# Sums for the second feed-forward products formed during the first ones, stored and loaded into place

## The chip, the cores and the metric

The kernel runs on one core of a Trainium2 chip. The metric is the device time of one execution in microseconds (us). Engines are named as in the profile: PE (TensorE matmul), PEld (its weight load), DVE (VectorE), ACT (ScalarE), POOL (GpSimd), SP (SyncE, which here only issues transfers). A name ending in q (SPq, DVEq) is an engine's queue of instructions.

## The reference, cut to what matters

Two transformer blocks follow each other on 1024 tokens of width 1024, in fp32. Each ends in a gated feed-forward network, and only these two networks are touched here. `D_FF` is 2816.

```python
def _swiglu(h, w_ffn_in, w_ffn_out):
    a, g = jnp.split(h @ w_ffn_in, 2, axis=-1)
    return (jax.nn.silu(g) * a) @ w_ffn_out
...
        x = x + g2 * _swiglu(_modulate(_rmsnorm(x, norm2_g[l]), sh2, sc2), w_ffn_in[l], w_ffn_out[l])
```

## The kernel before

**Products.** Every fp32 product is made of three fp32r matmuls: an operand x is split into a high part (a cast, made by ACT at L192) and a low part (x minus the high part, made by DVE or POOL at L193), and high by high, high by low and low by high are added in PSUM. PSUM has eight banks, used in turn, four named `mm` and four named `ax`. A 512-token product of one 128-row column is 128x512 in size; q is 0 or 1 for the two halves of the tokens.

**First products** (`ffn_in`, L1021). The hidden width is 22 columns f of 128 rows. A column and its gate form a 2x2 block product by Strassen's scheme in Winograd's form: seven products of 12 matmuls, in the order B11, T2, T1, T3, T4, B21, B22, with sums of weights on DVE (`total`, L1036) and sums of results on DVE (L1123 to L1129). `hidden` (L1072) multiplies the two factors into one 128x512 tile for each f and q, and `store` and `flush` (L220, L225) put it out to the DRAM tensor `hid` on SP's queue, 44 stores in each feed-forward.

**Second products** (`ffn_out`, L1132). The 22 columns are taken in five blocks, `FF_BLOCKS = (("P", 3), ("W", 6), ("P", 3), ("W", 6), ("P", 4))`. A P block is plain: 16 products of 3 (or 4) columns, 9 matmuls each for three columns. A W block is again Strassen-Winograd over six columns, in three pairs (k, k+3): 28 products of 9 matmuls (L1270 to L1272), seven for each pair of output rows m. P blocks evacuate PSUM with ACT (the first block, L1316) or with a DVE addition into x (L1281, in the second feed-forward L1279); W blocks with DVE (L1325 to L1333, L1281) and some with POOL.

**Operands of the second products.** A generator prepares each block's operands during the block before; `tick` runs it one step per product. For a P block it is `plain` (L1143): load a tile of `hid` (L1149), split it. For a W block it is `forms` (L1155). It loads the pair's four tiles b11, b12, b21, b22 into temporaries (L1169) and forms, on DVE except for T3 on POOL,

```python
T1 = b12 - b11    # L1179      T3 = b22 - b12   # L1180, POOL
T2 = b22 - T1     # L1182      T4 = T2 - b21    # L1187
```

and splits B11, B21, B22 and T1 to T4 into the parts that the matmuls read: `half` tiles for B11 and most of B21, the pool `hl` of 32 buffers for the rest. So W block 1 is prepared in P block 0, and W block 3 in P block 2. The weights of the second products are loaded by `unit` (L148, split at L150 and L151) or, for W blocks, by `supply` (loads L1233, DVE sums L1243 to L1246, splits L192 and L193). During W block 3, `residue` adds the residual from DRAM on DVE (L1288); during W block 1 of the first feed-forward some constants of the attention are made (`extra`, L1531 to L1541).

**Order.** Each engine runs its instructions in order. A list scheduler decides that order when the kernel is built, so a queue's order can differ from the order of the code.

## Time and profile before

| | us |
|---|---|
| median of 3 runs | 3383.36 (3383.23 to 3383.85) |
| the profiled execution | 3384.4 |
| its span | 3382.5 |
| PE busy in it | 3238.6 (96%) |
| DVE, POOL, ACT busy | 2135.1, 1533.4, 1357.7 |
| first feed-forward: first products, then the five blocks | from about 1191, 1622 to 1867 |
| second feed-forward: first products, then the five blocks | from about 2684, 3115 to the end |

PE is busy nearly always, so what can be won without taking away matmuls is the time in which it waits or runs at less than its usual pace. "Busy" counts instructions from start to end, and matmuls overlap; how many matmuls ran in a stretch, beside how long it is, shows more than the busy share. All times below count from the start of the span.

### The profile page before, as it was taken

What the parts mean: (1) busy time and instruction counts of PE and PEld (TensorE: products, weight loads), DVE (VectorE), ACT (ScalarE), POOL (GpSimd) and SP (SyncE); (2) the same over time, 40 slices, a digit from 0 to 9 for tenths busy, and PEclk for the clock granted to TensorE, in tenths of its full rate; (3) what the DMA queues carried; (4) which work ended last, traced back from release to release, by engine and by line L of the source; (5) the groups of instructions that cost most, each with busy time, mean ns of one, the idle gap of its engine ahead of it and who ended that gap; (6) DMA issues with size and microseconds to landing.
All of it is one profiled execution on the core that took longest, in us unless ns stands there. A gap on an engine that the chain in (4) does not pass through costs nothing. (4 is left out here: it accounts for less than half of the span.)

```text
span 3382.5 us, 43295 instructions
## 1 busy us (share of the span) xinstructions
PE 3238.6 (96%) x15868; PEld 2690.6 (80%) x15868; DVE 2135.1 (63%) x3438; ACT 1357.7 (40%) x2394; POOL 1533.4 (45%) x991
## 2 busy tenths in 40 slices
PE   7989999999999999999999999999999999999988
PEld 4779888888988878888777878787877878888767
DVE  7563234234577386555698578778776586564786
ACT  4552122221122342323433377767675332232433
POOL 3213233231322685454565534444445675544865
PEclk8989999999999999999999999999999999999999
DMA  7121111244237422221443411112114422222342
GB/s 272 60 103 54 63 57 60 75 163 152 79 100 234 154 84 99 78 78 68 129 138 118 133 33 52 55 47 63 58 50 147 143 100 94 87 78 94 101 139 72
DMA packets 153012, 335.11 MB, mean 99 GB/s; under 512 B 20864, under 2 KB 29184, under 8 KB 152800
## 3 DMA queue, kind: packets, MB, share of 16 engines
q1 hardware_dynamic: 140640, 311.36, 27.8%
q10 hardware_dynamic: 12160, 20.98, 1.7%
q8 instruction: 126, 2.06, 0.3%
q14 instruction: 86, 0.70, 0.1%
HBM read 263.07 MB, written 69.21 MB: 98 GB/s over the span
## 5 line engine op out<-in xcount | busy, mean ns | idle before, releaser
L151 POOL TENSOR_TENSOR wl<-raw,wh 128x1024 fp32r<-128x1024 f32 (+1 forms) x188 | 421.9, 2247 | 707.9 <-ACT wh L150 645.9
L163 PE MATMUL mm<-hl,wh 128*128 128x512 f32 (+1 forms) x1584 | 629.8, 398 | 1.4 <-ACT t L1567 1.4
L164 PE MATMUL mm<-hl,wh 128*128 128x512 f32 (+1 forms) x1584 | 618.9, 391 | 0.0
L165 PE MATMUL mm<-hl,wl 128*128 128x512 f32 (+1 forms) x1584 | 618.5, 390 | 0.0
L193 POOL TENSOR_TENSOR wl<-half,wh 128x512 fp32r<-128x512 f32 x308 | 431.7, 1424 | 346.8 <-ACT wh L192 341.5
L150 ACT CAST wh<-raw 128x1024 fp32r<-128x1024 f32 (+3 forms) x189 | 177.1, 939 | 453.4 <-PE mm L164 340.8
L165 PEld LDWEIGHTS mm<-hl,wl 128*128 128x128 f32 (+1 forms) x1584 | 297.2, 188 | 64.3
L163 PEld LDWEIGHTS mm<-hl,wh 128*128 128x128 f32 (+1 forms) x1584 | 297.7, 188 | 59.3 <-ACT t L1567 1.8
L164 PEld LDWEIGHTS mm<-hl,wh 128*128 128x128 f32 (+1 forms) x1584 | 298.0, 188 | 56.7 <-issue 0.5
L192 ACT CAST wh<-half 128x512 fp32r<-128x512 f32 x308 | 178.5, 618 | 392.0 <-PE ax L1058 197.1
L1036 DVE TENSOR_TENSOR half<-half 128x512 f32<-128x512 f32 x176 | 204.4, 1201 | 3.0
L1626 POOL TENSOR_SCALAR p<-p,ast 128x384 f32<-128x384 f32 (+1 forms) x64 | 82.5, 1289 | 240.4 <-DVE ast L1624 160.9
L175 PE MATMUL mm<-wh,hl 128*128 128x256 f32 x576 | 165.2, 287 | 0.0
L176 PE MATMUL mm<-wh,hl 128*128 128x256 f32 x576 | 163.7, 285 | 0.8 <-DVE hl L193 0.6
L177 PE MATMUL mm<-wl,hl 128*128 128x256 f32 x576 | 163.5, 284 | 0.0
L1058 PE MATMUL mm<-hl,wh 128*128 128x512 f32 x360 | 140.5, 390 | 3.3 <-POOL hl L193 3.3
L1057 PE MATMUL mm<-hl,wh 128*128 128x512 f32 x360 | 140.3, 390 | 0.7 <-ACT hl L192 0.7
L1059 PE MATMUL mm<-hl,wl 128*128 128x512 f32 x360 | 140.1, 389 | 0.0
L1057 PE MATMUL ax<-hl,wh 128*128 128x512 f32 x344 | 134.2, 390 | 2.1 <-ACT hl L192 1.3
L1059 PE MATMUL ax<-hl,wl 128*128 128x512 f32 x344 | 134.1, 390 | 0.1
L1058 PE MATMUL ax<-hl,wh 128*128 128x512 f32 x344 | 133.9, 389 | 0.0
L193 POOL TENSOR_TENSOR wl<-raw,wh 128x384 fp32r<-128x384 f32 x96 | 120.1, 1273 | 17.9 <-ACT wh L192 17.9
(412 smaller groups left out, 7992.4 us busy)
## 6 DMA issues: line engine op xcount, KB each, us to landing
half<-in_w_fi SPq DMA_DIRECT2D x196, 256.0 KB, 4.8
hid<-t SPq DMA_DIRECT2D x78, 256.0 KB, 2.0
half<-hid SPq DMA_DIRECT2D x72, 256.0 KB, 4.9
raw<-in_w_ada SPq DMA_DIRECT2D x32, 512.0 KB, 3.8
raw<-in_w_o SPq DMA_DIRECT2D x32, 512.0 KB, 3.7
raw<-in_w_fo SPq DMA_DIRECT2D x32, 384.0 KB, 3.8
slot<-in_w_ada SPq DMA_DIRECT2D x16, 512.0 KB, 10.2
raw<-in_w_u SPq DMA_DIRECT2D x16, 512.0 KB, 3.9
```

Source lines behind the costliest of these rows:

```text
L150: nc.scalar.copy(hi, r)
L151: self.last_split = (eng or nc.gpsimd).tensor_tensor(lo, r, hi.bitcast(F32), op=ALU.subtract).ins
L163: mm(o, wh[:, k], h[k][q][:, s], start=k == 0, stop=False)
L164: mm(o, wh[:, k], l[k][q][:, s], start=False, stop=False)
L165: mm(o, wl[:, k], h[k][q][:, s], start=False, stop=k == kt - 1)
L175: mm(o, h[k][q][:, s], wh[:, k % 4], start=k == 0, stop=False)
L192: self.nc.scalar.copy(hi, x)
L193: (eng or self.nc.vector).tensor_tensor(lo, x, hi.bitcast(F32), op=ALU.subtract)
L1036: V.tensor_tensor(s, a, b, op=op)
L1057: mm(o, wh[:, k], h, start=k == 0, stop=False)
L1058: mm(o, wh[:, k], l, start=False, stop=False)
L1059: mm(o, wl[:, k], h, start=False, stop=k == 3)
```

## The change

`ffn_in` now takes the columns of a W block pair by pair (3 and 6, 4 and 7, 5 and 8, then 12 and 15 and so on: `order`), keeps the four tiles of a pair, and as soon as the second column is done forms T1, T2 and T4 on DVE and T3 on POOL. These sums go to a new DRAM tensor `sums`. All stores of hidden tiles and sums are issued by ACT, one per product, at least one entry behind (`due`); b12 of a pair isn't stored, since only the sums use it. `forms` no longer adds anything: it loads B11, B21, B22 and T1 to T4 straight into the buffers of their low parts, and `split` takes the high part from there and then the low part in place. The pool of `half` tiles grows from 44 to 47 buffers. The products, their operands and their number stay the same (15273 PE instructions in both programs), as do the counts of DVE and POOL instructions (3440 and 996). DMAs issued by ACT rise by 124, those of SP fall from 954 to 902.

```diff
--- before.py
+++ after.py
@@ -1018,7 +1018,7 @@
                 nc.scalar.dma_start(self.xs[m][:, hs(q)], x[m][q])
             self.bg.append(norm(q, acc))
 
-    def ffn_in(self, wi, hid):
+    def ffn_in(self, wi, hid, sums):
 
 
         nc = self.nc
@@ -1026,9 +1026,20 @@
         add, sub = ALU.add, ALU.subtract
         nf = FT
 
+        order, pair, f0 = [], {}, 0
+        for kind, n in FF_BLOCKS:
+            if kind == "W":
+                for k in range(n // 2):
+                    order += [f0 + k, f0 + n // 2 + k]
+                    pair[f0 + n // 2 + k] = f0 + k
+            else:
+                order += range(f0, f0 + n)
+            f0 += n
+        held, due = {}, deque()
+
         def load(f, i, j):
             r = self.half()
-            nc.sync.dma_start(r, wi[2 * f + i][:, hs(j)])
+            nc.sync.dma_start(r, wi[2 * order[f] + i][:, hs(j)])
             return r
 
         def total(a, b, op):
@@ -1050,6 +1061,8 @@
         def product(w, n):
             mm = nc.tensor.matmul
             self.tick()
+            if len(due) > 1:
+                nc.scalar.dma_start(*due.popleft())
             banks[0] += 1
             o = self.mm_bank() if banks[0] % 2 else self.ax_bank()
             wh, wl = w
@@ -1070,8 +1083,21 @@
             return s
 
         def hidden(f, q, s, c):
+
             V.tensor_tensor(s, s, c, op=ALU.mult)
-            self.store(hid[f][:, hs(q)], s)
+            f = order[f]
+            held[f, q] = s
+            if not (f in pair.values() and q):
+                due.append((hid[f][:, hs(q)], s))
+            if f in pair and q:
+                g = pair[f]
+                b11, b12, b21, b22 = (held.pop(k) for k in ((g, 0), (g, 1), (f, 0), (f, 1)))
+                t1, t2, t4 = (self.half() for _ in range(3))
+                V.tensor_tensor(t1, b12, b11, op=sub)
+                nc.gpsimd.tensor_tensor(b12, b22, b12, op=sub)
+                V.tensor_tensor(t2, b22, t1, op=sub)
+                V.tensor_tensor(t4, t2, b21, op=sub)
+                due.extend((sums[g][i], t) for i, t in enumerate((t1, t2, b12, t4)))
 
         raws, todo, ready = {}, [], deque()
         seen = [0]
@@ -1128,8 +1154,10 @@
             hidden(f, 0, s0, u3)
             V.tensor_tensor(u2, u2, product(weights(), "B22"), op=add)
             hidden(f, 1, gate(u2), c22)
-
-    def ffn_out(self, wo, hid, xs, scale, pieces, squares, norm, extra=lambda: iter(())):
+        while due:
+            nc.scalar.dma_start(*due.popleft())
+
+    def ffn_out(self, wo, hid, sums, xs, scale, pieces, squares, norm, extra=lambda: iter(())):
 
 
 
@@ -1162,33 +1190,33 @@
                     X[nm].append((new(F32R), new(F32R)))
 
             def load(k):
-                B = []
-                for f in (k, n + k):
-                    for q in QS:
-                        B.append(self.t512() if k % 2 else self.half())
-                        nc.sync.dma_start(B[-1], hid[f0 + f][:, hs(q)])
-                return B
-            B = [load(k) for k in range(min(n, 2))]
+
+                for nm, f, q in (("B11", k, 0), ("B22", n + k, 1), ("B21", n + k, 0)):
+                    nc.sync.dma_start(X[nm][k][1].bitcast(F32), hid[f0 + f][:, hs(q)])
+                    if nm == "B22":
+                        nc.sync.dma_start(X["T1"][k][1].bitcast(F32), sums[f0 + k][0])
+                for i, nm in ((1, "T2"), (2, "T3"), (3, "T4")):
+                    nc.sync.dma_start(X[nm][k][1].bitcast(F32), sums[f0 + k][i])
+
+            def parts(k, nm, eng=None):
+                hi, lo = X[nm][k]
+                self.split(hi, lo, lo.bitcast(F32), eng=eng)
+            for k in range(min(n, 2)):
+                load(k)
             yield
             for k in range(n):
-                b11, b12, b21, b22 = B.pop(0)
-                parts = lambda nm, t, eng=None: self.split(*X[nm][k], t, eng=eng)
-                parts("B11", b11)
-                parts("B22", b22, nc.gpsimd)
+                parts(k, "B11")
+                parts(k, "B22", nc.gpsimd)
                 yield
-                V.tensor_tensor(b11, b12, b11, op=sub)
-                nc.gpsimd.tensor_tensor(b12, b22, b12, op=sub)
-                parts("T1", b11)
-                V.tensor_tensor(b22, b22, b11, op=sub)
+                parts(k, "T1")
                 yield
-                parts("B21", b21)
-                parts("T2", b22)
+                parts(k, "B21")
+                parts(k, "T2")
                 yield
-                V.tensor_tensor(b21, b22, b21, op=sub)
-                parts("T3", b12, nc.gpsimd)
-                parts("T4", b21)
+                parts(k, "T3", nc.gpsimd)
+                parts(k, "T4")
                 if k + 2 < n:
-                    B.append(load(k + 2))
+                    load(k + 2)
                 yield
 
         def block(bi):
@@ -1351,15 +1379,16 @@
 
     def ffn(self, wi, wo, *a):
         hid = self.dram(f"hid{self.loads}", [FT, P, T])
-        self.ffn_in(wi, hid)
-        self.ffn_out(wo, hid, self.xs, *a)
+        sums = self.dram(f"sums{self.loads}", [FT, 4, P, HQ])
+        self.ffn_in(wi, hid, sums)
+        self.ffn_out(wo, hid, sums, self.xs, *a)
 
     def block1(self):
         with ExitStack() as ctx:
             self.banks(ctx, 4, 4, "1")
             self.ap = self.pool(ctx, "ada", 2)
             self.phase_a()
-            self.gp = self.pool(ctx, "halves1", 44)
+            self.gp = self.pool(ctx, "halves1", 47)
             a = self.spatial()
             self.merge1(*a)
             self.lru_consts()
@@ -1792,7 +1821,7 @@
         self.mixers()
         with ExitStack() as ctx:
             self.banks(ctx, 4, 4, "3")
-            self.gp = self.pool(ctx, "halves2", 44)
+            self.gp = self.pool(ctx, "halves2", 47)
             self.merge2()
             self.ffn(self.I["w2_fi"], self.I["w2_fo"], None,
                      [(0, slice(0, HQ)), (1, slice(0, 256)), (1, slice(256, HQ))],
```

The order of SP's queue at the end of the first products of the first feed-forward, before: the hidden stores (L225) stand between loads of weights (`in_w_fo`), of block 0's tiles (L1149) and of the forms' temporaries (L1169).

```order
L225 DMA hid_9260<-t_12572 128x512
L148 DMA raw<-in_w_fo 128x384 x2
L1149 DMA half<-hid_9260 128x512
L148 DMA raw<-in_w_fo 128x384
L1149 DMA half<-hid_9260 128x512 x2
L225 DMA hid_9260<-t_12664 128x512
L1169 DMA t_12810<-hid_9260 128x512
L1169 DMA t_12812<-hid_9260 128x512
L1149 DMA half<-hid_9260 128x512
L225 DMA hid_9260<-t_12681 128x512
```

And of the change, at the same place (`in_w_fi` are the weights of the first products; L1195, L1197 and L1199 load the forms of block 1, L1177 the tiles of block 0):

```order
L1042 DMA half<-in_w_fi 128x512 x88
L1195 DMA hl<-hid_9260 128x512
L1197 DMA hl<-sums_9261 128x512
L1199 DMA hl<-sums_9261 128x512 x3
L1195 DMA hl<-hid_9260 128x512
L1197 DMA hl<-sums_9261 128x512
L1199 DMA hl<-sums_9261 128x512 x3
L148 DMA raw<-in_w_fo 128x384 x2
L1195 DMA hl<-hid_9260 128x512
L1177 DMA half<-hid_9260 128x512
L1197 DMA hl<-sums_9261 128x512
L1195 DMA hl<-hid_9260 128x512
```

No store stands here any more, and ten of the forms' loads, into `hl` buffers, stand ahead of block 0's tiles. PE's order differs only in the first part of block 0 of each feed-forward.

The order of DVE in the second P block (block 2) of the first feed-forward, before; L1281 empties PSUM, L1179, L1182 and L1187 are sums of the forms, L193 makes low parts:

```order
L1281 SCALAR_TENSOR_TENSOR half<-mm,mod,half 128x512
L1179 TENSOR_TENSOR t_13718<-t_13720,t_13718 128x512
L193 TENSOR_TENSOR half<-t_13722,half 128x512
L1281 SCALAR_TENSOR_TENSOR half<-ax,mod,half 128x512
L1182 TENSOR_TENSOR t_13724<-t_13724,t_13718 128x512
L193 TENSOR_TENSOR hl<-t_13718,hl 128x512
L1187 TENSOR_TENSOR t_13722<-t_13724,t_13722 128x512
L1281 SCALAR_TENSOR_TENSOR half<-mm,mod,half 128x512
L193 TENSOR_TENSOR hl<-t_13724,hl 128x512
L193 TENSOR_TENSOR half<-half 128x512
L1281 SCALAR_TENSOR_TENSOR half<-ax,mod,half 128x512
```

And of the change, where L1309 is what L1281 was:

```order
L1309 SCALAR_TENSOR_TENSOR half<-mm,mod,half 128x512
L193 TENSOR_TENSOR hl<-hl 128x512
L193 TENSOR_TENSOR half<-half 128x512
L1309 SCALAR_TENSOR_TENSOR half<-ax,mod,half 128x512
L193 TENSOR_TENSOR hl<-hl 128x512 x2
L1309 SCALAR_TENSOR_TENSOR half<-mm,mod,half 128x512
L193 TENSOR_TENSOR half<-half 128x512
L193 TENSOR_TENSOR hl<-hl 128x512 x2
L1309 SCALAR_TENSOR_TENSOR half<-ax,mod,half 128x512
```

The sums between the evacuations are gone, the low parts of the same forms stay, now from an `hl` buffer into itself.

The sums' new place on DVE is in the first products (L1087 is the product in `hidden`, L1149 to L1155 sums of results, L1047 of weights):

```order
L1096 TENSOR_TENSOR half<-t_10370,t_10352 128x512
L1150 TENSOR_TENSOR half<-half,mm 128x512
L1152 TENSOR_TENSOR half<-half,ax 128x512
L1087 TENSOR_TENSOR t_10496<-t_10496,half 128x512
L1155 TENSOR_TENSOR half<-half,mm 128x512
L1087 TENSOR_TENSOR t_10520<-t_10520,half 128x512
L1098 TENSOR_TENSOR half<-t_10520,half 128x512
L1099 TENSOR_TENSOR half<-half,t_10496 128x512
L1047 TENSOR_TENSOR half<-half 128x512 x4
```

T1 (L1096) stands some instructions ahead of the others; T2 and T4 (L1098, L1099) follow the pair's last hidden tile and stand ahead of the sums of weights of a later column.

## Rows read from the trace of the kernel before

**Rows 1.** The page: busy time, share of the span and instructions of each engine.

```profile
PE 3238.6 (96%) x15868; PEld 2690.6 (80%) x15868; DVE 2135.1 (63%) x3438; ACT 1357.7 (40%) x2394; POOL 1533.4 (45%) x991
```

**Rows 2.** Stretches, first feed-forward: length, PE, PEld, DVE, ACT, POOL busy, clock, DMA.

```profile
1400.00:1600.00 200.00, 200.00 (x884) 165.65 (x883) 114.10 (x135) 57.92 (x103) 101.08 (x74) 1.00 0.22 75
1622.00:1658.00 36.00, 33.92 (x145) 26.50 (x144) 17.39 (x18) 18.82 (x35) 20.34 (x16) 1.00 0.57 181
1658.00:1672.00 14.00, 8.99 (x29) 6.19 (x28) 12.77 (x16) 10.73 (x21) 7.60 (x7) 0.88 0.00 0
1672.00:1728.00 56.00, 53.67 (x228) 43.40 (x227) 53.52 (x69) 16.56 (x35) 36.25 (x30) 0.97 0.42 135
1728.00:1766.00 38.00, 34.21 (x145) 26.30 (x143) 34.56 (x40) 14.01 (x27) 23.95 (x17) 1.00 0.49 155
1766.00:1797.00 31.00, 25.06 (x97) 18.58 (x98) 30.55 (x42) 9.33 (x20) 17.68 (x13) 0.96 0.45 153
```

**Rows 3.** The same view, of the second feed-forward.

```profile
3115.00:3150.00 35.00, 33.70 (x147) 27.00 (x146) 17.53 (x19) 17.96 (x35) 19.07 (x15) 1.00 0.58 186
3150.00:3164.00 14.00, 9.93 (x28) 6.61 (x27) 13.07 (x15) 9.77 (x21) 9.40 (x7) 0.76 0.00 1
...
3215.00:3252.00 37.00, 33.79 (x145) 26.38 (x143) 30.54 (x38) 11.86 (x24) 24.93 (x18) 1.00 0.41 133
3252.00:3281.00 29.00, 23.29 (x95) 17.21 (x96) 25.16 (x33) 9.54 (x20) 16.64 (x14) 1.00 0.50 160
```

**Rows 4.** Waits of PE, 1622 to 1728 us: total, times, longest.

```profile
PE ax L1271 <- DVE hl L193: 2.2, 1, 2.2
...
PE ax L1270 <- ACT hl L192: 1.7, 1, 1.7
```

**Rows 5.** Timeline of PE at the first sum-and-difference block's start.

```profile
1669.29 0.63 PE L1271 MATMUL mm<-hl,wh 128*128 128x512 f32 x1
1669.72 0.63 PE L1272 MATMUL mm<-hl,wl 128*128 128x512 f32 x1
```

**Rows 6.** Timeline of DVE, two rows: start, length, instruction, idle before.

```profile
1639.69 1.27 DVE L193 TENSOR_TENSOR half<-half 128x512 fp32r<-128x512 f32 x1 [7.38 <-ACT half L192]
...
1668.62 3.22 DVE L193 TENSOR_TENSOR hl<-half,hl 128x512 fp32r<-128x512 f32 x2
```

**Rows 7.** Timeline of PE: last matmul of the third block.

```profile
1764.20 0.39 PE L165 MATMUL ax<-half,wl 128*128 128x512 f32 x1
```

**Rows 8.** Timeline of DVE: last addition of that block.

```profile
1788.85 0.74 DVE L1281 SCALAR_TENSOR_TENSOR half<-ax,mod,half 128x512 f32<-128x512 f32 x1
```

**Rows 9.** Stretches, DVE's time on L1179, then L1182, then L1187 alone.

```profile
1728.00:1797.00 69.00, 2.54 (x3) 0.98 0.47 154
...
1728.00:1797.00 69.00, 3.66 (x3) 0.98 0.47 154
...
1728.00:1797.00 69.00, 2.04 (x3) 0.98 0.47 154
```

**Rows 10.** Waits of DVE, 1728 to 1797 us.

```profile
DVE half L1179 <- DMA half<-hid: 1.4, 1, 1.4
...
DVE half L1182 <- POOL half L1180: 0.7, 1, 0.7
DVE t L1182 <- POOL t L1180: 0.5, 1, 0.5
```

**Rows 11.** Groups of DVE in the first products, 1400 to 1600 us.

```profile
L1036 DVE TENSOR_TENSOR half<-half 128x512 f32<-128x512 f32 x40 | 46.9, 1212 | 0.8
...
L1036 DVE TENSOR_TENSOR half<-half,ax 128x512 f32<-128x512 f32 x17 | 11.7, 687 | 34.0 <-PE ax L1059 33.8
```

**Rows 12.** Waits of SP's queue over the whole span.

```profile
SPq L225 <- DVE t L1073: 551.2, 78, 15.8
```

**Rows 13.** The stored hidden rows: issues, length in ns; landing of all their transfers.

```profile
L225 SPq DMA_DIRECT2D hid<-t x78: 319/326/327, 1249.8 to 3117.2; - x78
...
DMA to landing us min/median/max: 2.0/2.8/7.4
```


## The prediction

> **What bounds the kernel now.** I read the page first: PE is busy 96% of the span [rows 1], so the only time to win is time in which PE waits or runs at its lower pace. That share hides which stage loses it, so I cut the two feed-forwards into stretches and counted matmuls in each. In the steady part of the first products 884 matmuls fill 200.00 us with no gap [rows 2]: 0.2262 us each. The loss of any other stretch is its length minus its matmuls times 0.2262. First feed-forward [rows 2]: block 0 (1622 to 1658) 36.0 − 145 × 0.2262 = 3.2; the start of W block 1 (1658 to 1672) 14.0 − 29 × 0.2262 = 7.4; the rest of it 4.4; block 2 (1728 to 1766) 5.2; the start of W block 3 (1766 to 1797) 9.1. Sum 29.3 us. Second feed-forward [rows 3]: block 0 1.7, start of block 1 7.7, block 2 4.2, start of block 3 7.5; sum 21.1. Together some 50 us, and this is where the change works. (Records missing from the trace can shift a stretch by some tenths.)
>
> Then I asked what each stretch waits for. At the start of block 1 the waits of PE name forms' splits: a low part on DVE 2.2 us, a high part on ACT 1.7 [rows 4]. Behind these waits some matmuls start 0.43 us apart in place of 0.23 [rows 5]; the granted clock of the stretch is 0.88, and 0.76 in the second feed-forward [rows 2, 3]. So part of these 7.4 and 7.7 us is PE at the lower of its two clocks (1.2 GHz) after having waited: it goes if the waits go. The forms are late because DVE starts on them only at 1639.69, after 7.38 us without work, and has the last two low parts at 1668.62 + 3.22 = 1671.8 [rows 6], 14 us after PE reached the block. In that time DVE is busy 12.77 of 14.00 us [rows 2].
>
> At the start of block 3 it is another wait: DVE is behind in emptying PSUM. It is busy 34.56 of 38.00 us in block 2 and 30.55 of 31.00 after it [rows 2]. PE's last matmul of block 2 starts at 1764.20 [rows 7], and DVE's last addition of that block ends at 1788.85 + 0.74 = 1789.6 [rows 8], about 25 us later. Eight banks of 9 matmuls cover 8 × 9 × 0.2262 = 16.3 us of lag; the 8.7 us over that is the stretch's 9.1 us.
>
> **The change part by part.** *Start of block 1.* The nine sums of a P block leave it, and with them the chain of DVE, POOL and DVE again by which one pair's forms followed the other. What stays is splits alone. Their loads stand on SP ahead of block 0's tiles, and the sums they read were stored long before (landing of a stored or loaded tile: median 2.8, longest 7.4 us [rows 13]). They need an `hl` buffer that PE has released, so they come one after the other with the last column's products (a column takes 84 × 0.2262 = 19 us), some 16 to 3 us before 1622. In the order the first splits on DVE then stand ahead of the last column's evacuations, some 20 us ahead of 1639.69. All but B11's and B21's, whose loads come last, should be ready when PE comes to block 1. I take 1 us left of each of the 7.4 and 7.7: **13 us**. Bounds: 5, if the last loads keep a part of the waits and so the lower clock, and 15.1.
>
> *Blocks 2 and 3.* In the first feed-forward the nine sums there take 2.54 + 3.66 + 2.04 = 8.2 us of DVE [rows 9], and DVE sits idle for them at least another 1.4 + 0.7 us, for a tile of `hid` and for POOL's T3 [rows 10]: 10.3 us. DVE is the late one there, so each microsecond comes off the lag, and the lag is what PE pays for. Blocks 2 and 3 lose 5.2 + 9.1 = 14.3; 4 remain by that sum. I take 9.5 of the 10.3, for DVE's other waits can grow. In the second feed-forward DVE is less full, 30.54 of 37.00 and 25.16 of 29.00 [rows 3], so part of the freed time falls on idle time: of a loss of 11.7 I take 7.5. Together **17 us**. Bounds: 0, if every freed microsecond is lost again to waits for the new loads, and 26.
>
> *Block 0 and the end of block 1.* The first lose 3.2 and 1.7, mostly to the last tiles' splits, which stay; the end of block 1 loses 4.4 while DVE is busy 53.52 of 56.00 us [rows 2], and the first forms of block 3 stand among that work. I take 1 + 2 = **3 us**; bounds 0 and 9.
>
> *The sums in the first products.* 36 additions on DVE and 12 on POOL come in. An addition of two SBUF tiles takes 1.21 us there, one that reads PSUM 0.69 [rows 11], so a pair costs DVE 3 × 1.21 = 3.6 us in two columns of 38 us, of which DVE is busy 57% (114.10 of 200) [rows 2]. That leaves 16 us free for 3.6, and T1 can run early. POOL is busy 101.08 of 200, and one addition per pair is added. PE's 200.00 of 200.00 shows that it never waited for either: cost 0, upper bound 12 pairs × 3.6 = 43 us if each addition holds PE up in full. I take 0, since the nearest row, the first products themselves, has room four times over.
>
> The Trainium skill, GPSIMD Engine Reference, section Key points, says that GpSimd shares its SBUF interfaces with VectorE, so that DVE instructions with two SBUF inputs are disturbed. Rows 11 agree: 1.21 against 0.69 us. By that rule the sums cost more in their new place, beside POOL's splits, than the 0.69 of an undisturbed one, 43 against 25 us of DVE; either fits into the free time, and the sum of the terms is the same.
>
> *Stores.* 88 issues of 0.326 us leave SP and 124 join ACT [rows 13], 40 us of ACT in all, in stretches in which it is busy 57.92 of 200 [rows 2]. What leaves SP is more than the issues: its queue stood 551 us before these stores, waiting for the tile [rows 12], and block 0's loads wait behind them. I give this no term of its own; it is how the loads above can leave early.
>
> The Trainium skill, DMA: Bandwidth & Descriptors, section Issuing engines are not separate DMA queues, says that transfers from different engines share the same 16 DMA engines, and that another issuer saves only issue time. That would make this part worth nothing to PE; the trace shows a wait in order on SP, not a lack of bandwidth (DMA share 0.22 in the first products), and a term of zero suits both.
>
> *New waits.* Loads into `hl` buffers hold SP until PE has released them, and weights of the next block stand behind them. Bounds: 0, and one late landing of at most 7.4 us [rows 13] at each of the four W blocks, 30. I take 2 us, near the low end, since the order puts these loads behind products that run long before the block.
>
> **Sum.** 13 + 17 + 3 − 2 = 31 us. 3384.4 of the profiled execution becomes 3353.4; the median of runs lies 1.0 below it, so 3352.4.
>
> **Rivals.** *DVE stays the bound* (0.17). From 1658 to 1833 DVE does work for nearly all of the time, and with 10.3 us less it may still be behind at block 3: the splits in place cluster behind their loads, and the lag returns. Then only the start of block 1 is won: 3383.4 − 13 = 3370. For it: 53.52 of 56.00 in block 1. Against it: the lag exceeds what the banks cover by only 8.7 us.
>
> *All is won* (0.07). If the waits of blocks 0 to 3 go altogether, 50 − 2 = 48 us: 3335. Against it: block 0's own last tiles and the weights' splits remain.
>
> *Slower: the new sums hold up the first products* (0.08). They stand in DVE's queue ahead of the sums of weights; if these make splits late by more than the seven products of weights that are kept ready (7 × 12 × 0.2262 = 19 us), or ACT stands at a store whose sum isn't done, PE waits in a stretch which now loses nothing. It decides from 31 / 12 = 2.6 us a pair; at the full 3.6 us, 43 − 31 makes 3395. Against it: PE has no wait at all there, with DVE at 57%.
>
> *Nothing happens* (0.06): the loads wait for their buffers so long that the splits are as late as now, and the lag goes on: 3383.
>
> **How the numbers follow.** The forecast, 0.62, has its own range of 3340 to 3363. With the partial rival at 3370 and most of the full one the range is 3338 to 3372, which leaves out the last two rivals and an end of the full one, some 0.18. A measurement of this kernel can tell about 0.2%, 6.8 us. Faster by more than that: 0.62 + 0.17 + 0.07 = 0.86; within it 0.06; slower 0.08.
>
> **What would show it.** Right: no wait of PE for an `hl` split at block 1's start and a clock near 1.00 there; the first `hl` splits on DVE before 1622; DVE's last addition of block 2 no more than some 17 us after PE's last matmul of it; 200.00 of 200.00 in the first products with DVE near 125. Wrong: gaps of PE in the first products for weights' splits; PE waiting at block 0 or 1 for a load that stood behind a buffer; DVE as full in block 2 as now.

## The result and the profile after

The changed kernel takes 3336.46 us (median of 4 runs, 3333.26 to 3337.94) against 3383.3 (4 runs, 3376.93 to 3383.85): ratio 0.9865, interval 0.9853 to 0.9878, 46.8 us faster. A gain of 31 was forecast; the time lies 1.5 us under the range, beside the number of the rival "All is won" (3335, chance 0.07). The profiled execution took 3337.94.

The page's line of busy times, to be read with [rows 1]: every engine runs as many instructions as before, and PE's share is 97%.

```profile
PE 3221.1 (97%) x15868; PEld 2686.4 (81%) x15868; DVE 2129.2 (64%) x3438; ACT 1362.0 (41%) x2394; POOL 1535.1 (46%) x991
```

The stretches of the first feed-forward, the columns those of [rows 2]:

```profile
1410.00:1610.00 200.00, 200.00 (x884) 165.64 (x884) 115.66 (x143) 60.72 (x108) 108.00 (x77) 1.00 0.28 93
1619.00:1655.00 36.00, 33.92 (x146) 26.79 (x145) 23.09 (x22) 25.06 (x47) 22.79 (x18) 1.00 0.46 151
1655.00:1669.00 14.00, 14.00 (x64) 11.58 (x63) 8.76 (x12) 7.17 (x14) 9.72 (x10) 1.00 0.43 133
1669.00:1712.00 43.00, 43.00 (x191) 35.63 (x190) 41.93 (x58) 11.99 (x24) 24.37 (x21) 1.00 0.43 140
1712.00:1746.00 34.00, 33.57 (x146) 26.88 (x145) 31.33 (x36) 14.75 (x28) 19.77 (x14) 1.00 0.82 285
1746.00:1775.00 29.00, 26.06 (x109) 19.92 (x109) 28.72 (x38) 9.55 (x20) 19.29 (x15) 1.00 0.47 148
```

And of the second, as in [rows 3]:

```profile
3087.00:3124.00 37.00, 34.25 (x146) 26.69 (x146) 22.30 (x22) 23.90 (x48) 22.76 (x18) 1.00 0.47 151
3124.00:3138.00 14.00, 14.00 (x63) 11.58 (x63) 8.07 (x11) 6.78 (x14) 10.90 (x10) 1.00 0.37 128
3181.00:3213.70 32.70, 32.70 (x146) 27.09 (x145) 32.18 (x41) 10.57 (x21) 20.40 (x14) 1.00 0.69 235
3213.70:3242.00 28.30, 28.30 (x127) 23.43 (x126) 23.68 (x30) 9.81 (x21) 23.98 (x19) 1.00 0.38 121
```

The start of block 1, 14 us in which PE ran 29 and 28 matmuls before, now runs 64 and 63 at a clock of 1.00. Block 2 and the start of block 3 have no loss left in the second feed-forward; in the first, 1746 to 1775 still loses 29.0 − 109 × 0.2262 = 4.3 us. The first products run 884 matmuls in 200.00 us as before, with DVE at 115.66 (125 was expected). Not that the sums are cheap: the nine of three pairs take 2.1 + 4.8 + 5.0 = 11.9 us there. But 40 sums of weights take 39.9 us in place of 46.9 [rows 11], and the products in `hidden` (L1087, before L1073) 0.81 us each in place of 0.95:

```profile
L1047 DVE TENSOR_TENSOR half<-half 128x512 f32<-128x512 f32 x40 | 39.9, 1038 | 0.5
L1099 DVE TENSOR_TENSOR half<-half,t 128x512 f32<-128x512 f32 x3 | 5.0, 1665 | 0.1
L1098 DVE TENSOR_TENSOR half<-t,half 128x512 f32<-128x512 f32 x3 | 4.8, 1593 | 0.3
L1096 DVE TENSOR_TENSOR half<-t,t 128x512 f32<-128x512 f32 x3 | 2.1, 684 | 0.0
```

To place the microseconds, I took the start of each stage's first matmul in the profiled execution of each kernel (found by counting matmuls, 15868 in each) and subtracted. "ahead" is all before the first products of the first feed-forward, b0 to b4 are the blocks. Each row is one execution, which can lie some us off its kernel's median (e3: 3372.04 against 3377.34; e4: 3349.24 against 3342.9).

```
                          ahead |  first    b0    b1    b2    b3    b4 |  first    b0    b1    b2    b3
before                   1190.6 |  431.6  36.2  69.7  38.2  66.5  61.1 |  431.3  34.7  65.2  37.2  65.6
after                    1187.7 |  431.6  35.9  57.3  33.8  61.6  57.3 |  431.5  36.8  57.1  32.4  57.3
e1_no_sums               1189.6 |  431.6  34.6  62.1  37.4  59.4  57.3 |  431.3  35.0  57.1  33.5  60.5
e2_stores_act            1189.1 |  431.6  37.1  69.1  38.8  65.6  61.2 |  431.3  36.7  64.0  37.6  64.9
e3_adds_back             1186.9 |  431.6  35.2  67.6  33.0  70.3  57.4 |  431.5  37.0  67.3  32.4  65.7
e4_stores_sp             1190.6 |  431.6  39.0  57.3  34.8  63.5  57.3 |  431.5  39.1  57.1  32.4  57.7
e5_pure_load             1188.2 |  431.6  44.3  57.3  34.3  67.4  57.3 |  431.5  43.9  57.1  32.4  61.7
e6_sums_twice            1190.1 |  431.7  36.2  57.3  32.4  61.4  57.3 |  431.5  36.1  57.1  32.4  57.4
e7_temporaries           1190.7 |  431.6  35.5  60.4  35.5  61.0  57.4 |  431.5  37.5  57.3  32.4  59.4
e8_plain_inplace         1189.4 |  431.6  37.5  57.3  32.4  59.2  57.3 |  431.5  38.2  57.1  32.4  57.9
e9_residue_half          1187.5 |  431.6  35.9  57.3  34.9  62.7  57.3 |  431.5  37.3  57.1  32.4  59.6
e10_residue_pool         1188.9 |  431.7  36.4  57.3  34.3  67.5  57.3 |  431.5  37.4  57.1  32.4  62.9
e11_before_residue_half  1187.3 |  431.6  35.7  68.7  38.5  70.8  57.3 |  431.3  35.7  64.8  38.0  66.1
e12_unchained            1187.6 |  431.6  34.5  67.8  36.9  69.7  57.3 |  431.2  34.3  63.8  33.8  67.1
e13_before_no_residue    1186.6 |  431.6  35.6  68.7  39.0  58.0  57.4 |  431.3  35.1  64.9  36.0  60.2
e14_after_no_residue     1192.2 |  431.6  36.6  57.3  32.8  58.0  57.3 |  431.5  36.2  57.1  32.4  57.3
e15_no_pool_sum          1189.1 |  431.6  33.7  68.3  34.3  69.5  57.3 |  431.3  34.1  62.0  35.2  65.8
e16_residue_late         1192.1 |  431.6  37.0  57.3  34.0  61.0  62.3 |  431.6  36.2  57.1  32.4  57.3
e17_before_residue_late  1189.3 |  431.6  35.7  68.8  39.8  63.0  66.8 |  431.3  35.2  64.7  36.5  65.6
```

From before to after: ahead −2.9; first feed-forward b0 −0.3, b1 −12.4, b2 −4.4, b3 −4.9, b4 −3.8; second b0 +2.1, b1 −8.1, b2 −4.8, b3 −8.3. Blocks 0 to 3 give 41.1 us, where the medians differ by 46.8.

On DVE, low parts into `hl` are made from 1609.47 on, in the last column of the first products, and in a row from 1624.37; before, DVE's first form came at 1639.69 [rows 6].

```profile
1609.47 3.39 DVE L193 TENSOR_TENSOR hl<-hl 128x512 fp32r<-128x512 f32 x3 [2.83 <-ACT hl L192]
...
1624.37 8.52 DVE L193 TENSOR_TENSOR hl<-hl 128x512 fp32r<-128x512 f32 x5
...
1639.19 1.50 DVE L193 TENSOR_TENSOR half<-half 128x512 fp32r<-128x512 f32 x1 [5.70 <-ACT half L192]
```

In block 3 of the first feed-forward PE's remaining waits are for DVE's evacuations and a weights' high part:

```profile
PE ax L1298 <- DVE half L1309: 1.2, 1, 1.2
PE mm L1298 <- ACT wh L192: 1.0, 1, 1.0
```

### The profile page after: what moved, and what is told of

Read it like the earlier page. It is cut to its first block, busy times and chain, and to the rows that moved or that the text cites. A ratio compares the mean times of both kernels' runs of the same rounds, so it can differ in the third digit from the quotient of the medians.

```text
span 3336.2 us, 43488 instructions
## 1 busy us (share of the span) xinstructions
PE 3221.1 (97%) x15868; PEld 2686.4 (81%) x15868; DVE 2129.2 (64%) x3438; ACT 1362.0 (41%) x2394; POOL 1535.1 (46%) x991
## 5 line engine op out<-in xcount | busy, mean ns | idle before, releaser
L193 POOL TENSOR_TENSOR wl<-half,wh 128x512 fp32r<-128x512 f32 x308 | 435.3, 1436 | 317.2 <-ACT wh L192 306.4
L1047 DVE TENSOR_TENSOR half<-half 128x512 f32<-128x512 f32 x176 | 180.0, 1063 | 2.5 <-issue 0.4
L193 POOL TENSOR_TENSOR wl<-raw,wh 128x384 fp32r<-128x384 f32 x96 | 116.0, 1226 | 40.0 <-ACT wh L192 40.0
```

Of the source, the lines that this page charges most:

```text
L193: (eng or self.nc.vector).tensor_tensor(lo, x, hi.bitcast(F32), op=ALU.subtract)
L1047: V.tensor_tensor(s, a, b, op=op)
```

## The experiments

Each time below is a median in us. The ratio behind it is to runs of before on the same chip, with its 95% interval. The median of before itself differs by some 3 us between these sets, so smaller differences to the change (3336.46, 0.9865) say little. The table above has the stages of each.

**Theory A**: the sums cost the time, by what they take on DVE and POOL in the P blocks (load) or by the waits from engine to engine (chain). **Rival R**: the transfers gain it (stores off SP, forms loaded early and into place).

**e1: before, sums left out.** `T1` to `T4` are split from the tiles as loaded.

```diff
-                V.tensor_tensor(b11, b12, b11, op=sub)
-                nc.gpsimd.tensor_tensor(b12, b22, b12, op=sub)
...
-                V.tensor_tensor(b22, b22, b11, op=sub)
...
-                V.tensor_tensor(b21, b22, b21, op=sub)
```

> The kernel before with the twelve sums of each W block left out of the forms: T1 to T4 are split from the loaded tiles as they are, so the output is not the reference's. Stores, loads, splits and the order of PE are unchanged. Theory A (the cost was the sums themselves, their time on DVE and POOL and the chain from one engine to the other, in the P blocks): blocks 0 to 3 lose about 40 us less, 3340 to 3350. Rival R (the gain came from the transfers: stores off SP's queue, forms loaded earlier and into place): no more than 10 us, 3373 or above.

3341.91 us, 0.9882 (0.9867 to 0.9897): 39 us of the 47 without the sums and nothing else; R is refuted as the main cause. In blocks 0 to 3 it is 33.7 of the 41.1 (3.8 of the 39 lie in block 4). This run has the old 44 `half` buffers, so the three more that the change has can be worth no more than a part of the rest; no run has them alone. By stage: block 1 −7.6 and −8.1, block 2 −0.8 and −3.7, block 3 −7.1 and −5.1.

DVE comes to the forms as late as before, and still the start of block 1 loses nothing: 64 matmuls in 14.00 us at a clock of 1.00.

```profile
1638.79 1.27 DVE L193 TENSOR_TENSOR half<-half 128x512 fp32r<-128x512 f32 x1 [7.70 <-ACT half L192]
```

```profile
1655.80:1669.80 14.00, 14.00 (x64) 11.59 (x63) 11.78 (x12) 8.57 (x18) 13.93 (x11) 1.00 0.27 87
```

In block 1 of the first feed-forward 4.8 us more go with the full change; PE's waits in blocks 0 and 1 of e1 show what stays, a wait at the end of block 1 for DVE (L1327), which is still in arrears:

```profile
PE mm L1270 <- DVE t L1327: 1.8, 1, 1.8
PE ax L164 <- POOL half L193: 0.6, 1, 0.6
```

**e2: before, stores on ACT.**

```diff
-            self.store(hid[f][:, hs(q)], s)
+            due.append((hid[f][:, hs(q)], s))
```

`product` issues `due` on ACT, one entry per product, as in the change.

> The kernel before with only its 88 hidden stores moved from SP's queue to ACT's, one per product. Theory A: within 5 us of before, 3378 to 3385. Rival R: most of the gain, 3345 to 3360, because block 0's loads no longer wait behind stores.

3384.28, 1.0009 (1.0 to 1.0018). Nothing is won.

**e4: the change, stores on SP.**

```diff
-                nc.scalar.dma_start(*due.popleft())
+                nc.sync.dma_start(*due.popleft())
```

> The changed kernel with its 124 stores on SP's queue, at the same places in the code. Theory A: within 4 us of the change, 3333 to 3341, for nothing in the blocks waits for a store. Rival R: loads stand behind stores again, waits return at the start of blocks 0 and 1, 3346 to 3365.

3342.9, 0.9888 (0.9873 to 0.9903): some 6 us slower than the change, between A's band and R's; the intervals of the two ratios overlap a little. In the profiled execution 3.1 and 2.3 of it lie in block 0, 1.9 in block 3 and 2.9 ahead of the feed-forwards; block 1 is as fast as in the change.

The Trainium skill, DMA: Bandwidth & Descriptors, section Issuing engines are not separate DMA queues, has the move save issue time alone. e2 agrees, with 1.0009. e4 differs by some 6 us; whether by issue time or by order on SP, these runs don't separate.

**e3: the change, sums put back with the results thrown away.**

```diff
+            def again(k, a, b, eng=V):
+                eng.tensor_tensor(self.half(), X[a][k][1].bitcast(F32), X[b][k][1].bitcast(F32), op=sub)
...
+                again(k, "B11", "T1")
+                again(k, "B22", "T3", nc.gpsimd)
...
+                again(k, "B22", "T2")
...
+                again(k, "B21", "T4")
```

> The changed kernel with additions of the sums' number and size put back into the forms (nine on DVE and three on POOL per W block), their results thrown away, so that nothing waits for them. Theory A in the form of the lag (each microsecond on DVE in block 2 makes PE wait in block 3): about 16 of the 22 us won in blocks 2 and 3 go, block 1 stays won, 3350 to 3356. Theory A in the form of the chain (what cost time was the waiting of one engine for the next, not DVE's time): 3336 to 3341. Rival R: 3336 to 3341 too.

3377.34, 0.9989 (0.9979 to 0.9998): nearly all of the gain is gone, more than either form of A said. This was not the pure load that I meant it to be. The additions read B11's low part, whose `half` buffer is loaded late; in DVE's queue all later low parts stood behind that wait, and PE waited 8.4 us at the start of block 1. By stage, block 1 loses 10.3 and 10.2 to the change and block 3 8.7 and 8.4. DVE's timeline, then PE's wait:

```profile
1637.06 1.51 DVE L193 TENSOR_TENSOR half<-half 128x512 fp32r<-128x512 f32 x1 [8.40 <-ACT half L192]
1638.60 1.67 DVE L1206 TENSOR_TENSOR half<-half,hl 128x512 f32<-128x512 f32 x1
```

```profile
PE mm L1306 <- DVE half L193: 8.4, 1, 8.4
```

So low parts that stand behind a late tile can cost what the change won. In before they stand behind one too [rows 6], but e1 keeps that wait and has only 4.8 us more in block 1 than the change.

**e5: the change, the same load in place.** Each low part of T1 to T4 is written once more on its engine.

```diff
+                if nm in ("T1", "T2", "T3", "T4"):
+                    (eng or V).tensor_tensor(lo, lo.bitcast(F32), lo.bitcast(F32), op=ALU.add if eng else ALU.max)
```

> The changed kernel; each low part of T1, T2 and T4 is written once more by DVE (the maximum of the tile with itself) and that of T3 by POOL (the tile added to itself, so T3's low part is doubled and the output is not the reference's). That is the number, size and place of the sums of before, without a chain between engines or a wait for another tile. Lag (DVE's time itself costs PE's time in blocks 2 and 3): W block 3 and block 2 lose 14 to 18 us of the two feed-forwards again, block 1 at most 3, 3351 to 3356. Chain (what cost time was that one engine waited for the other and for late tiles): no more than 5 us over the change, 3336 to 3342.

3363.32, 0.9938 (0.9921 to 0.9955): 27 us lost, outside both bands. Block 3 loses 5.8 and 4.4, as the load theory has it though less than I said, and block 1 nothing. Unforeseen: block 0 loses 8.4 and 7.1, for the extra work now stands ahead of block 0's last tiles on DVE. Once PE has stood for 4.86 us its next matmuls start 0.43 us apart:

```profile
1640.52 0.79 PE L164 MATMUL ax<-half,wh 128*128 128x512 f32 x1 [4.86 <-DVE half L193]
...
1641.54 0.63 PE L164 MATMUL ax<-half,wh 128*128 128x512 f32 x1
1641.97 0.63 PE L165 MATMUL ax<-half,wl 128*128 128x512 f32 x1
```

**e6: the change, each sum in the first products twice.**

```diff
+                for t, eng in ((t1, V), (t2, V), (t4, V), (b12, nc.gpsimd)):
+                    eng.tensor_tensor(t, t, t, op=ALU.max if eng is V else add)
```

> The changed kernel with a second instruction of the same size behind each sum in the first products (maximum of the tile with itself on DVE; on POOL T3 is added to itself, so T3 is doubled and the output is not the reference's). My price of the sums in the first products was 0: then the first products keep their 431.6 and 431.5 us and the whole stays within 3 us of the change, 3334 to 3340. Rival: they already cost something there, or are near the point where they do: each pair 1 us or more, 3348 or above.

3335.08, 0.9856 (0.9841 to 0.9871). Twice the sums cost the first products 0.2 us at most (431.7 and 431.5 us, before 431.6 and 431.3); PE stays at 200.00 with DVE at 123.99:

```profile
1410.00:1610.00 200.00, 200.00 (x884) 165.59 (x884) 123.99 (x153) 59.97 (x107) 113.16 (x80) 1.00 0.26 88
```

**e7: the change, forms loaded into temporaries.**

```diff
-                self.split(hi, lo, lo.bitcast(F32), eng=eng)
+                self.split(*X[nm][k], got.pop(nm), eng=eng)
+                more()
```

`more` issues the next load, into a `half` tile; six are issued ahead.

> The changed kernel with the forms loaded into half tiles, six ahead, and split from there, in place of loads into the low parts' buffers. If only the sums and their chain matter: within 5 us of the change, 3334 to 3342. If the loads straight into the low parts matter, because they need no temporary and so come before block 0's tiles: the start of block 1 loses up to 8 us in each feed-forward again, 3345 to 3353.

3348.12, 0.989 (0.9876 to 0.9905). Block 1 loses 3.1 and 0.2, block 2 1.7 in the first, block 3 2.1 in the second; 3.0 lie ahead of the feed-forwards, where the kernels are alike. Loads into place are worth some 7 us in these stages, but fewer at block 1 than I allowed.

**e8: the change, block 0's tiles in place too.**

```diff
-                    t = self.half()
-                    nc.sync.dma_start(t, hid[f0 + f][:, hs(q)])
+                    nc.sync.dma_start(lo.bitcast(F32), hid[f0 + f][:, hs(q)])
...
-                    self.split(hi, lo, t, eng=nc.gpsimd if i % 2 else None)
+                    self.split(hi, lo, lo.bitcast(F32), eng=nc.gpsimd if i % 2 else None)
```

> The changed kernel with the P blocks' tiles too loaded into their low parts and split in place, one half tile fewer for each. If block 0's tiles are late for want of half tiles, their loads come earlier and block 0 loses 2 to 5 us less over both feed-forwards: 3330 to 3334. If they are late for their place on SP behind the forms: the same as the change, 3335 to 3338.

3340.3, 0.9874 (0.9859 to 0.9888). Block 0 is not shorter (37.5 and 38.2 us against 35.9 and 36.8), so a `half` tile more or less is not what it waits for.

**e12: before, sums of the same size without a chain.**

```diff
-                V.tensor_tensor(b11, b12, b11, op=sub)
-                nc.gpsimd.tensor_tensor(b12, b22, b12, op=sub)
+                V.tensor_tensor(b11, b11, b11, op=ALU.max)
+                nc.gpsimd.tensor_tensor(b12, b12, b12, op=add)
```

and so for the other two.

> The kernel before with each sum replaced by an instruction of the same size on the same engine that reads one tile alone (maximum of the tile with itself on DVE, the tile added to itself on POOL), so the output is not the reference's. DVE and POOL do the same work at the same places; no sum waits for another engine or another tile. Chain theory: most of what the run without sums won comes, 30 us or more: 3345 to 3353. Load theory: at most 5 us: 3376 to 3383. Both, as the changed kernel with the load put back suggests (block 3 lost again, block 1 not): block 1 gains 8 to 15 us, blocks 2 and 3 little, 3365 to 3373.

3374.21, 0.9981 (0.9972 to 0.9991): some 6 us, between the bands of load alone and of both. Block 1 gains 1.9 and 1.4 where e1 gained 7.6 and 8.1; block 3 is even longer (69.7 and 67.1). Not every wait between engines is gone: `b22` is still overwritten (L1182) after POOL has read it for B22's low part, and each split still waits for its own DVE instruction. But the waits of DVE's sums for POOL ahead of block 1 fall from 5.0 to 1.2 us in the first feed-forward and from 3.8 to none in the second. The largest of them before, and what is left:

```profile
DVE half L1182 <- POOL hl L193: 2.4, 1, 2.4
```

```profile
DVE t L1182 <- POOL hl L193: 1.2, 1, 1.2
```

So the load, not the chain, is most of it. PE's waits at block 1 are still there:

```profile
PE mm L1270 <- DVE t L1327: 1.8, 1, 1.8
PE mm L1271 <- DVE half L193: 1.7, 1, 1.7
PE ax L1270 <- ACT wh L192: 1.4, 1, 1.4
```

**e15: before, POOL's sum left out** (`b12` is split as loaded).

```diff
-                nc.gpsimd.tensor_tensor(b12, b22, b12, op=sub)
```

> The kernel before with T3's subtraction on POOL left out (T3 is split from b12 as loaded, so the output is not the reference's); the nine sums of DVE stay. If the step through POOL is what holds the chain up (DVE waits 0.7 to 2.4 us for POOL ahead of each T2): 10 us or more faster, 3365 to 3373. If it is DVE's own time and the late tiles: no more than 5, 3378 to 3384.

3371.21, 0.9965 (0.9952 to 0.9978): 10 us, in the band that I had set for the step through POOL. This run takes away that step and POOL's work together and can't tell them apart. e12 takes away the step alone and gains less (the intervals overlap a little), which speaks for POOL's work, without showing it. Block 1 −1.4 and −3.2, block 2 −3.9 and −2.0, block 3 none in the second and +3.0 in the first.

**e13 and e14: the residual's additions left out, before and after.**

```diff
-                    V.tensor_tensor(was[0], was[0], was[1], op=add)
+                    pass
```

> The kernel before without the sixteen additions of the residual in each feed-forward; they are left out altogether, so the output is not the reference's; their loads stay. Load theory: 14.7 us of DVE's time at the start of block 3 go and its loss of 9.1 and 7.5 us with them; 3365 to 3370. If DVE's time is not what delays block 3: 3379 to 3384.

> The changed kernel without the additions of the residual, left out as in the run on the kernel before. Load theory: block 3 of the first feed-forward comes down from 61.6 to about 57.3 us, nothing else moves: 3331 to 3334. If its rest is waits for weights' splits: 3335 to 3338.

e13: 3361.31, 0.9942 (0.9927 to 0.9957); 13.9 of the 20 us lie in block 3 (−8.5 and −5.4), with all sums in place. e14: 3335.35, 0.9856 (0.984 to 0.9873), which can't be told from the change (its runs go from 3328.68 to 3340.17); in its profiled execution block 3 of the first feed-forward falls from 61.6 to 58.0. By the stages, DVE's time at that place is PE's. PE's largest waits in blocks 2 and 3 of e13:

```profile
PE mm L165 <- POOL wl L151: 2.3, 3, 1.1
PE mm L1270 <- DVE half L1281: 1.8, 1, 1.8
```

**e9, e10, e11, e16, e17: the residual elsewhere.** The first line added is that of e9 (on the change) and e11 (on before), the second that of e10; the move below is that of e16 (on the change) and e17 (on before).

```diff
-                    V.tensor_tensor(was[0], was[0], was[1], op=add)
+                    (nc.gpsimd if q else V).tensor_tensor(was[0], was[0], was[1], op=add)
+                    nc.gpsimd.tensor_tensor(was[0], was[0], was[1], op=add)
...
-            if bi == 3:
-                self.bg.append(residue())
             self.bg.append(nxt[1])
+            if bi == 3:
+                self.bg.append(residue())
```

> The changed kernel with every second addition of the residual (eight of sixteen in each feed-forward) on POOL in place of DVE. PE's order is the same. Lag theory: block 3 of the first feed-forward, the one place where PE still waits for DVE's evacuations, loses 2 to 4 us less (61.6 to about 58.5); the second has nothing left to win: 3331 to 3335. Rival: block 3's remaining loss is POOL's and ACT's weights' splits, which get later: 3336 to 3342.

> The changed kernel with all sixteen additions of the residual on POOL. Lag theory: as with the half, and block 3 of the first feed-forward near 57.3: 3330 to 3334. Rival: POOL, busy 60% there, makes the weights' low parts late: block 3 longer than with the half, 3336 to 3345.

> The kernel before with every second addition of the residual on POOL; about 7 us of DVE's time at the start of block 3 go, the sums stay. PE's order is the same as before. Lag theory (DVE's time at the end of block 2 and the start of block 3 is PE's): block 3 loses 5 to 7 us less in the first feed-forward and 3 to 6 in the second, blocks 0 to 2 stay: 8 to 12 us faster than before, 3371 to 3375. Chain theory (the forms' waits are what counts, not DVE's time): no more than 3 us faster.

> The changed kernel with the residual's additions taken up behind the last block's tiles during block 3, not ahead of them. PE's order is the same, DVE's and POOL's work too. Lag theory: at the start of block 3 DVE has four low parts to make where it had some ten additions, its lag falls under what the banks cover, block 3 of the first feed-forward goes from 61.6 to about 58, the rest stays: about 3 us under the change, 3331 to 3335. If the lag only moves to the end of block 3, or the last block's tiles don't matter: the same as the change, 3335 to 3339.

> The kernel before with the same move of the residual's additions. Lag theory: block 3 loses 6 to 8 us less in the first feed-forward and 3 to 5 in the second, as in the run without these additions: 3367 to 3373, without any change to the sums. If it is the sums' own place that counts: no more than 3 us, 3378 to 3383.

None of them won: e9 3339.6, 0.9873 (0.9858 to 0.9888); e10 3349.73, 0.9906 (0.9891 to 0.9921); e11 3380.35, 0.9995 (0.9986 to 1.0005); e16 3347.4, 0.9894 (0.9879 to 0.9909); e17 3384.57, 1.0006 (0.9997 to 1.0016). The expectations by the lag were wrong in all five: the work cost as much elsewhere. On POOL it made the weights' low parts late; PE waited for them in e10, and in block 3 of e11, which fell in the band of the chain for this reason:

```profile
PE mm L1300 <- POOL wl L193: 5.7, 4, 1.9
```

```profile
PE mm L1272 <- POOL wl L193: 4.5, 3, 2.1
```

Put off, it made block 4 longer (62.3 and 66.8 us) by more than block 3 won (0.6 and 3.5). No version tried is faster than the change beyond doubt.

## Why the prediction fell short

- **What bounds the kernel**: right. The stretches named lost some 50 us, and blocks 0 to 3 gave back 41.1.
- **Sums in the first products at 0**: right, shown by e6. DVE's sign there, near 125, did not come: 115.66.
- **Blocks 2 and 3, first feed-forward**: right in size, 9.5 forecast, 4.4 + 4.9 = 9.3 measured. e13 shows that DVE's time there is PE's; e5 that the sums' load there costs 5.8. But the working holds only in part, and the match of the numbers is partly luck. DVE's last addition of block 2 was to come no more than 17 us after PE's last matmul of it (1745.70); it ends at 1768.5, 23 us later where it was 25 before [rows 7, 8], and PE still loses 4.3. DVE is as full in block 2 as before, 31.33 of 34.00 us against 34.56 of 38.00, which I had named as a sign of being wrong; the block is 4 us shorter all the same:

```profile
1767.78 0.74 DVE L1309 SCALAR_TENSOR_TENSOR half<-ax,mod,half 128x512 f32<-128x512 f32 x1
```

- **Blocks 2 and 3, second feed-forward**: the term failed in size, 7.5 against 13.1. I discounted freed time because DVE was less full there on average. e1 gives 8.8 for the sums alone, more than the 7.5 already. The other 4.3 came with the rest of the change; which part of it gave them, no run shows.
- **Start of block 1**: the largest miss, 13 + 2 (its end) against 12.4 + 8.1 = 20.5. I kept 1 us of wait at each start, for late B11 and B21, and half of the end's loss; all of it went. The explanation was wrong in part too. I named the chain, but e12 without most of it gives 3.3 and e1 without the sums 15.7. I named the late start of the forms at 1639.69, but e1 starts them as late and loses nothing at either start of block 1. It was the sums' work on DVE and POOL, as far as these runs show. And the waits for forms that I read [rows 4] are those of the first feed-forward; in the second PE waited longest for a weight's high part, whose cast stood in ACT's queue behind casts of forms, and one of these had stood for T4's sum (L1187):

```profile
PE ax L1270 <- ACT wh L192: 2.5, 1, 2.5
```

```profile
3150.61 0.62 ACT L192 CAST hl<-t 128x512 fp32r<-128x512 f32 x1 [1.69 <-DVE t L1187]
...
3154.41 0.51 ACT L192 CAST wh<-raw 128x384 fp32r<-128x384 f32 x1
```

The other 4.8 us lie at the end of block 1 in the first feed-forward: with the low parts made from 1609 on, DVE comes to block 1 with less in arrears, and the wait for L1327 there, which stays in e1 and e12, is gone.

- **Stores, no term of their own**: e2 bears this out for the stores alone. With loads into place, e4 has them cost some 6 us on SP.
- **Block 0 and new waits**: a gain of 1 and a loss of 2 were forecast. Block 0 became 0.3 us shorter in the first feed-forward and 2.1 longer in the second, and PE waits for no load into place. e5 shows why block 0 is the sore place: the forms' low parts stand ahead of its last tiles.
- **Outside blocks 0 to 3**, nothing was forecast, and 2.9 + 3.8 us came. The 2.9 can't be called an effect of the change: "ahead" goes from 1186.6 to 1190.6 among the kernels made from before and from 1186.9 to 1192.2 among those made from the change, with the same code there in each. The 3.8 in block 4 came in nearly all variants, also in e11, which keeps the sums; what made it is told below.

So 31 grew to 46.8 by 5.5 in block 1, 5.4 in blocks 2 and 3 and 5.7 outside these blocks (46.8 − 41.1), less 0.8 in block 0 and the waits together. Two steps failed. The first is the sizing of **Start of block 1** and of the second feed-forward's blocks 2 and 3: 13 + 2 and 7.5 were summed, 20.5 and 13.1 measured. By this alone the gain would be 41.1 and the time 3342, inside the range. The second is the time outside blocks 0 to 3, which the prediction put at nothing without a word; its 5.7 us carried the result out of the range. That the result stands beside "All is won" is partly luck, for that rival's case did not come in full: blocks 0 and 3 still lose.

## What to carry to other kernels

Count the matmuls in a stretch, not its busy share: the difference to the steady pace is the most that can be won there without taking away matmuls, and where one engine is in arrears, taking work from it can give back nearly all of it, with the clock back at 1.00. Before moving work, look for a stage with idle time on that engine (here the first products, where even twice the sums were free); moving it to another busy engine or a later stage brought the wait back there. An instruction put in as a pure load is one only if it waits for nothing that the kernel has late. A run that takes away an engine's work and a wait for it together can't say which of the two counted.

## What the runs showed of the hardware

In before, a DVE instruction of 8 columns took 2.32 us while POOL worked on two 128x1024 tiles, and PE then waited 1.99 us; DVE, POOL and PE in block 4 of before:

```profile
1862.88 2.32 DVE L262 TENSOR_SCALAR rsy<-ms 128x8 int32<-128x8 int32 x1
```

```profile
1860.43 4.74 POOL L151 TENSOR_TENSOR wl<-raw,wh 128x1024 fp32r<-128x1024 f32 x2 [10.10 <-ACT wh L150]
```

```profile
1869.31 1.67 PE L276 MATMUL ax<-ident,rsy 128*128 128x128 f32 x8 [1.99 <-DVE rsy L267]
```

The same instruction in the changed kernel took 1.22 us, beside a shorter POOL instruction, and the shortest of that line's 21 in before 0.158.

```profile
1837.59 1.22 DVE L262 TENSOR_SCALAR rsy<-ms 128x8 int32<-128x8 int32 x1
```

```profile
1837.49 1.30 POOL L240 TENSOR_TENSOR half<-half,t 128x512 f32<-128x512 f32 x1
```

It ended when POOL's instruction did: at 1865.20 where POOL's second tile ended at 1865.17, and at 1838.81 where POOL's addition ended at 1838.79. In all 19 kernels it ended 0.03 us behind the POOL instruction that ran beside it. Beside a 128x1024 subtraction it took 2.31 to 2.34 us, and PE then waited (before, e2, e16 and e17); beside the 128x512 addition it took 1.22 or 1.23 in the other 15, and PE did not wait for it.

This is the 3.8 us of block 4 in the first feed-forward: 2.1 us until PE goes on, the rest in the matmuls behind the wait, which start 0.43 us apart. Which of POOL's instructions the small one meets follows from when DVE comes to it; what shifts the two against each other from kernel to kernel, no run here settles, so this part of the gain is a chance of timing and not shown to be the sums' doing.
